# Moving the first half's large loads and one store from SyncE's DMA queue to ScalarE's

## The chip, the cores and the metric

The kernel runs on one core of one Trainium2 chip. A core has five instruction streams that run side by side and meet through semaphores: PE (TensorE, matrix products), DVE (VectorE), ACT (ScalarE), POOL (GpSimd) and SP (SyncE, which here does nothing but begin DMA transfers). Each stream executes its instructions strictly in the order in which the program has them. The metric is the device time of one execution in microseconds (us), lower is better. Three runs of the kernel before took 1967.37, 1973.29 and 1975.88 us.

## The reference

One layer, 4096 tokens of width 1024, batch 1. The token rows are normalised and modulated to `h`; one projection of `h` feeds three mixers side by side, whose outputs are gated, joined and projected back:

```
h = _rmsnorm(x, g_pre) * (1.0 + scale[:, None]) + shift[:, None]
proj = h @ w_in
...
attn = _sliding_window_attention(...)            # 8 query heads, 2 key heads, window 128, sinks
rwkv = _rwkv7_mixer(h, rr, rk, rv, ...)          # 4 heads of 64, delta rule, token by token
gla = _gla_mixer(h, gq, gkk, gv, ...)            # 4 heads, chunks
...
y = jnp.concatenate([attn, rwkv, gla], axis=-1) @ w_out
return x + gate[:, None] * _rmsnorm(y, g_post)
```

The RWKV mixer is a recurrence `S = S*w + (S @ -kk)(kk*a)^T + v k^T` over 4096 tokens. The kernel does it in chunks of 64 tokens; each chunk needs the inverse of a 64x64 triangular matrix for each head.

## The kernel before, in words

Tokens are handled in 16 tiles of 256. The program has two halves. The first half makes `h` of every tile, the RWKV and the GLA mixer, and on the side splits the weights of the second half into two 16-bit parts. The second half is attention, the gates and the output projection. `h` travels from the first half to the second through a scratch tensor in DRAM, `hscr`.

In the first half a tile passes through stages, several tiles being under way at once:

- `stage_a` loads the tile's token rows twice over: `xh`, 128 rows of 1024 at a time (512 KB, two per tile, one buffer), for the sums of squares that ACT makes, and `xt`, the same tokens with channels on the partitions (1 MB, one buffer). From `xt` ACT and DVE make `hT`, the two 16-bit halves of `h` (ACT writes the high half, DVE subtracts for the low half), and `hT` is stored to `hscr` (1 MB).
- `stage_p` projects `hT` on PE (tiles `pv`, `lp`, `zz`, `gqk`): this is most of PE's work.
- `stage_qa`, `stage_qb` and `stage_qc` build the triangular matrices `AT` and invert them. The 16x16 blocks on the diagonal go through DRAM to be laid out anew: eight transfers `adr<-AT` of 8 KB, two `AS<-adr` of 64 KB, then fifteen steps of substitution on DVE (`tsc`, `TT`), two `tdr<-TT` of 32 KB, eight `td<-tdr` of 8 KB, and then the products `Xp`, `Xq` on PE that assemble the inverse.
- `stage_q2` runs the recurrence over the tile's four chunks (`rp`, `up`, `yp`), with ACT copying `UV` between products.
- `stage_c` and `stage_g` prepare weights (`cs` loads, `wscr`, `woscr` stores, `gaw` loads).

The order of the instructions is not the order of the code. Every call goes through a recorder (`Lane`, line 352 is the line of the recorded call, so nearly all instructions bear it), and `Order.pin` then walks through the recorded steps with a table of costs, engine by engine, and fixes the order in which each engine executes them. A DMA step counts there as a step of SP with 0.47 us of SP's time and a landing time by size, all behind each other in one pipe. In the whole program all transfers but one are begun by SP, so they stand in one queue in the order of SP's stream; the one exception is a load of `gscr` at line 1598 that ACT begins at the start of the second half.

The scheduling framework gives every DMA step one of eight completion semaphores, in turn, whichever engine begins it. A step that is given a semaphore waits, before it is begun, until the step that had it last (eight DMA steps earlier) has landed. In the listings these waits read `DMAHW0_49` to `DMAHW7_49`; a wait for another engine's work bears that engine's name.

Of the kernel before, what the change touches and what calls it, by code (L numbers as in the profile page):

```python
# [21 lines left out]
P = 128  # L22
D = 1024
T = 4096
NT = 256
# [14 lines left out]
LANES = ((0.06, 1.04e-3, VL), (0.02, 1.0e-3, AL), (0.1, 2.3e-3, 0.0), (0.0, 1e-3 / 2.4, PL), (0.05, 0.0, 2.0))  # L40
# [3 lines left out]
HOP_FROM = {"PE": 0.037, "DVE": 0.034, "Activation": 0.034, "Pool": 0.06, "SP": 0.6}  # L44
HOP_INTO = {"PE": 0.02, "Pool": 0.04, "SP": 0.03}
# [20 lines left out]
class Order:  # L66
# [34 lines left out]
    def note(self, eng, name, outs, ins, func, r):  # L101

        st = Step()
# [3 lines left out]
        e, o = st.eng, outs[0]  # L107
# [3 lines left out]
        if e == "PE":  # L111
# [9 lines left out]
            cells = [4 * a + b for a in range(*rows) for b in range(*cs)]  # L121
            st.array = (mode, cells, 2 if f32 and name == "matmul" else 1, took, issue)
            st.occ = st.lat = 0.0
        elif e == "SP":
            st.bytes = math.prod(ins[0].shape) * SIZE[ins[0].dtype]
            kb = st.bytes / 1024
            st.occ = 0.47
            st.lat = next((t for k, t in ((8, 2.2), (64, 3.2), (128, 3.4), (256, 4.4), (512, 5.8)) if kb <= k), 7.5)
        elif e == "Activation":
            st.occ = (0.05 if on_psum else 0.093) + 0.093 * (len(ins) - 1) + 0.832e-3 * n  # L130
            st.lat = st.occ + 0.1
            if len(outs) > 1:
                st.occ += 0.187
                st.lat = st.occ + 0.02
            st.table = LN_TABLE if func == AF.Ln else EXP_TABLE if func in (AF.Exp, AF.Tanh) else None
        elif e == "Pool":
            if name == "memset":
                st.occ = 0.06
            elif name == "tensor_copy":
                st.occ = 0.25 if n <= 2 else 0.11 + 0.95e-3 * n  # L140
            elif n <= 8:
                st.occ = 0.33 + 0.165 * n
            else:
                st.occ = 0.42 + 1.5e-3 * n if n <= 512 else 1.85e-3 * n
            st.lat = st.occ + 0.05
        else:
            if name == "tensor_reduce":
                n = math.prod(ins[0].shape[1:])
            fast = name in ("tensor_scalar", "tensor_single_scalar") and not on_psum and o.dtype == F32
            fixed, rate = 0.065 + 0.06 * (cols > 0), 1.04e-3  # L150
            if fast:
                rate = 0.53e-3
            elif name == "transpose":
                fixed = 0.09
            elif name == "tensor_tensor_scan":
                rate = 2.08e-3
            elif name == "memset":
                fixed, rate = 0.05, 0.3e-3
            elif name == "tensor_tensor" and len(o.shape) == 3 and o.shape[2] <= 16 and n > 16:
                fixed, rate = 0.09, 1.55e-3  # L160
            st.occ = fixed + rate * n
            st.lat = st.occ + 0.085
# [7 lines left out]
            st.port = e == "Pool" and wide > 8  # L170
        k, st.needs, st.turn = len(self.steps), {}, []
        out_r, in_r = [self.region(a) for a in outs], [self.region(a) for a in ins]
        if e in ("Activation", "DVE"):

            st.half = (out_r[0][1], in_r[0][1] if e == "Activation" and in_r and out_r[0][2] - out_r[0][1] <= 64 else None)
        tiles = {a.tensor.name: a.tensor for a in [*outs, *ins]}

        if e == "SP" and self.behind is not None:
            st.turn.append(self.behind)

        def need(j, data=False):
# [51 lines left out]
    def pin(self):  # L233

        steps = self.steps
# [15 lines left out]
            if head[k] == k and not left[k]:  # L251
                ready[st.eng][k] = 0.0
        free = dict.fromkeys(ENGINES, 0.0)
        cells, mode, table, pipe, half = [0.0] * 16, None, None, 0.0, {}
        last, count, held = {}, 0, 0.0
        while count < len(steps):
            e = min((e for e in ENGINES if ready[e]), key=lambda e: max(free[e], min(ready[e].values())))
# [12 lines left out]
            for k in bursts.get(k, [k]):  # L270
# [10 lines left out]
                else:  # L281
# [9 lines left out]
                    free[e], st.end = t + st.occ, t + st.lat  # L291
                    if st.bytes:

                        pipe = max(pipe, t + 1.7) + st.bytes / 400e3
                        st.end = max(st.end, pipe)
                st.start = t
                if e in last:
                    self.tc.add_manual_dep(
                        st.ins, last[e], mybir.DependencyInfo(mybir.DependencyClass.NoSync, mybir.DependencyReason.DATA))
                last[e], count = st.ins.name, count + 1  # L300
                for q in st.then:
                    to, h = steps[q], head[q]
                    left[h] -= 1
                    at = t if k in to.turn else 0.0
                    if k in to.needs and e != to.eng:
                        at = max(at, st.end + HOP_FROM[e] + HOP_INTO.get(to.eng, 0.0))
                    elif k in to.needs and (e == "SP" or e != "PE" and to.needs[k]):
                        at = max(at, st.end + (1.2 if e == "SP" else 0.03))
                    when[h] = max(when[h], at)
                    if not left[h]:  # L310
                        ready[to.eng][h] = when[h]
# [105 lines left out]
def hybrid_kernel(ctx, tc, x, xc, rows, ada1, adaw, w1, wl, w2, wo, cst, abias, out):  # L417
# [4 lines left out]
    G = Lane(model, nc.gpsimd, *LANES[2])  # L422
    PE = Lane(model, nc.tensor, *LANES[3], serial=True)
    SP = Lane(model, nc.sync, *LANES[4])

    def pool_of(at, name, bufs=1, **kw):
        return model.order.pool(at.enter_context(tc.tile_pool(name=name, bufs=bufs, **kw)), bufs)
# [229 lines left out]
    with ExitStack() as p1:  # L657
# [60 lines left out]

        def load_tokens(i, a):
            xh = wt([P, D], "xh", 1)  # L720
            SP.dma_start(xh, x[i * NT + a * P : i * NT + (a + 1) * P, :])
            E[i]["xh"] = xh

        def load_channels(i):
            xt = E[i]["xt"] = t_x().rearrange("p a d -> p (a d)").rearrange("p (k t) -> p k t", k=KD)
            SP.dma_start(xt, xc[i])


        scolb = pp.tile([P, KD, 32], F32, name="scolb")
# [297 lines left out]
        def stage_a(i):  # L1027
# [26 lines left out]
            for kp in range(KD // 2):  # L1054
# [3 lines left out]
                S.activation(hT[:, 0, ks], xt[:, ks], AF.Identity)  # L1058
                V.tensor_sub(hT[:, 1, ks], xt[:, ks], hT[:, 0, ks])
                yield [xt]  # L1060
            SP.dma_start(hscr[i], hT.rearrange("p a k t -> p (a k t)"))

        def stage_p(i):

# [1147 lines left out]
```

## Time and profile before

| | before |
|---|---|
| three runs, us | 1967.37, 1973.29, 1975.88 |
| the profiled execution, its own time, us | 1972.81 |
| span of the profiled execution, first to last instruction, us | 1971.0 |
| PE busy in the span, us | 1875.8 (95%) |
| DVE, ACT, POOL busy, us | 1412.5, 1118.1, 375.2 |
| data moved by DMA, MB | 257.57 |

The first half occupies PE up to about 925 us of the span, the second half the rest; around the border the two overlap. In the listings of stretches, each row has a stretch of the span, its length, then for each engine its busy time and its number of instructions, then the granted clock of PE, the mean busy share of the 16 DMA engines, and the rate. In lists of waits a row says who waited, for what, and then the total, the number of waits and the longest. "SPq" and "ACTq" are the instructions by which SP and ACT begin a transfer.

### The profile page before, as it was taken

To read this page: it belongs to the slowest core of one execution; us is meant where nothing else is said; L and a number is where in the kernel's file an instruction comes from. 1 tells how busy PE (TensorE), PEld (TensorE's weight loads), DVE (VectorE), ACT (ScalarE), POOL (GpSimd) and SP (SyncE) were. 2 spreads that over 40 slices of the span, in tenths; PEclk is the share of its full clock that TensorE was granted. 3 is DMA by queue.
4 is the path that set the end of the run, shared out by engine and by line. 5 is a ranking of instruction groups with operands and counts; after the bars stand their busy time and mean duration, and the time that the engine had idled before them with its cause. 6 is when DMAs were issued, how large, how long until landed. Compare 5 with 4: busy or idle time off the path is not lost.

```text
span 1971.0 us, 59112 instructions
## 1 busy us (share of the span) xinstructions
PE 1875.8 (95%) x24651; PEld 1458.2 (74%) x24651; DVE 1412.5 (72%) x3919; ACT 1118.1 (57%) x2529; POOL 375.2 (19%) x549
## 2 busy tenths in 40 slices
PE   5799999999999999999999999999999999999997
PEld 1577788877878777877777777877778777777783
DVE  4777788888878888767638775667666676666756
ACT  4887787777777767645335443444444444344443
POOL 0533233543333344332200000000000000000001
PEclk9899999999999999999999999999999999999999
DMA  9553453443342443115244443244332444334415
GB/s 378 188 168 120 141 171 124 141 155 100 104 132 86 133 133 112 52 40 191 62 142 146 153 131 112 90 150 132 121 121 90 150 132 119 123 94 147 132 40 169
DMA packets 154264, 257.57 MB, mean 131 GB/s; under 512 B 49027, under 2 KB 100995, under 8 KB 147845
## 3 DMA queue, kind: packets, MB, share of 16 engines
q1 hardware_dynamic: 153844, 253.19, 40.2%
q8 instruction: 196, 3.21, 0.7%
q14 instruction: 80, 0.65, 0.1%
q10 hardware_dynamic: 144, 0.52, 0.1%
HBM read 192.83 MB, written 60.82 MB: 129 GB/s over the span
## 4 chain that ended last, share of the span: by engine, by line
PE 80%; DVE 6%; DMA 5%; ACT 5%; issue 3%; SPq 1%; POOL 1%; DVEq 0%; ACTq 0%; POOLq 0%
PE gp L352 17%; PE op L352 14%; PE zz L352 8%; PE qp L352 8%; PE pv L352 4%; PE lp L352 4%; PE gqk L352 3%; PE kp L352 3%; PE vp L352 2%; PE ovp L352 2%; PE sc L352 2%; PE atp L352 2%; PE yp L352 1%; PE rp L352 1%; DMA xh<-in_x 1%
## 5 line engine op out<-in xcount | busy, mean ns | idle before, releaser
L352 PEld LDWEIGHTS <-mtp 128*128 128x128 f16 x1344 | 129.2, 98 | 142.3 <-DMA ov<-woscr 3.6
L352 PE MATMUL op<-o,mtp 128*128 128x512 f16 x768 | 181.0, 380 | 0.0
L352 ACT ACTIVATE pr<-pr,nm,lsc 128x160 f32<-128x160 f32 (+2 forms) x256 | 129.1, 506 | 87.2 <-DVE nm L352 87.1
L352 PE MATMUL op<-ov,mtp 128*128 128x512 f16 x576 | 138.5, 382 | 3.8 <-DVE yv L352 2.4
L352 PEld LDWEIGHTS <-hT 128*128 128x128 f16 x1536 | 120.9, 100 | 23.8 <-ACT hT L352 4.1
L352 POOL TENSOR_TENSOR ry<-sy,expo 128x1 f32<-128x1 f32 x30 | 18.1, 619 | 537.6 <-DVE sy L352 537.6
L352 PE MATMUL pv<-gvh,hT 128*128 128x272 f16 x512 | 101.7, 290 | 5.7 <-ACT hT L352 4.0
L352 DVE TENSOR_TENSOR yv<-op,yv 128x512 f32<-128x512 f32 x105 | 70.6, 684 | 50.8 <-PE op L352 50.8
L352 DVE CUSTOM_DVE_ANT_0 pr<-sc,ab,kept 128x160 f32<-128x160 f32 (+2 forms) x256 | 85.6, 375 | 28.9 <-PE sc L352 28.8
L352 DVE SCALAR_TENSOR_TENSOR ag<-ag,gp 128x512 f32<-128x512 f32 x64 | 43.8, 684 | 80.3 <-ACT ag L352 80.1
L352 PE MATMUL gqk<-hT,gqkh 128*128 128x256 f16 x512 | 88.7, 275 | 6.6 <-DVE zb L352 6.1
L352 PE MATMUL zz<-hT,kh 128*128 128x256 f16 x512 | 94.3, 274 | 0.0
L352 PE MATMUL gp<-hT,q6h 128*128 128x256 f16 x512 | 88.7, 279 | 5.5 <-issue 5.5
L352 ACT ACTIVATE ag<-gp,gh 128x512 f32<-128x512 f32 x64 | 43.7, 683 | 88.3 <-PE gp L352 88.0
L352 PE MATMUL lp<-hT,Lh 128*128 128x256 f16 x512 | 93.4, 276 | 0.1
L352 PE MATMUL zz<-hT,rh 128*128 128x256 f16 x512 | 92.0, 275 | 0.7 <-DVE gq_s L352 0.7
L352 PE MATMUL gp<-hT,q5h 128*128 128x256 f16 x512 | 87.6, 274 | 0.0
L352 ACT ACTIVATE xt<-xt,sh,gs 128x256 f32<-128x256 f32 x128 | 70.0, 591 | 30.6 <-DVE xt L352 28.3
L352 PE MATMUL gp<-hT,q3h 128*128 128x256 f16 x512 | 87.2, 273 | 0.1
L352 PE MATMUL zz<-hT,vh 128*128 128x256 f16 x512 | 86.2, 273 | 0.0
L352 PE MATMUL qp<-hT,q0h 128*128 128x256 f16 x512 | 86.2, 273 | 0.0
L352 PE MATMUL gp<-hT,q4h 128*128 128x256 f16 x512 | 86.1, 273 | 0.0
(429 smaller groups left out, 5765.4 us busy)
## 6 DMA issues: line engine op xcount, KB each, us to landing
ov<-woscr SPq DMA_DIRECT2D x96, 512.0 KB, 5.1
xh<-in_x SPq DMA_DIRECT2D x32, 512.0 KB, 3.8
xt<-in_xc SPq DMA_DIRECT2D x16, 1024.0 KB, 8.2
hscr<-hT SPq DMA_DIRECT2D x16, 1024.0 KB, 5.6
hT<-hscr SPq DMA_DIRECT2D x16, 1024.0 KB, 4.9
x<-in_x SPq DMA_DIRECT2D x30, 512.0 KB, 4.3
out<-yv SPq DMA_DIRECT2D x30, 512.0 KB, 2.9
cs<-in_w SPq DMA_DIRECT2D x56, 256.0 KB, 4.3
```

The source lines that it names most:

```text
L352: r = f(*args, **kw)
```

## The change

The loads of `xh` and `xt` (except those of the first tile) and every store of `hscr` are begun by ACT. Nothing else of the work changes; the other transfers of the first half, those of the inverse among them, stay with SP. The planner is told of it: a DMA step begun by ACT takes its 0.47 us from ACT's time, and there are two pipes for landing times, one for SP's transfers and one for ACT's, that slow each other where they overlap. Since the planner walks through all steps with these costs, the order of every engine's instructions in the first half comes out anew. The second half's order is the same but for the steps of the first half that reach into it.

```
+    AQ = Lane(model, nc.scalar, *LANES[4])
...
         def load_tokens(i, a):
             xh = wt([P, D], "xh", 1)
-            SP.dma_start(xh, x[i * NT + a * P : i * NT + (a + 1) * P, :])
+            (AQ if i else SP).dma_start(xh, x[i * NT + a * P : i * NT + (a + 1) * P, :])
...
             xt = E[i]["xt"] = t_x().rearrange("p a d -> p (a d)").rearrange("p (k t) -> p k t", k=KD)
-            SP.dma_start(xt, xc[i])
+            (AQ if i else SP).dma_start(xt, xc[i])
...
-            SP.dma_start(hscr[i], hT.rearrange("p a k t -> p (a k t)"))
+            AQ.dma_start(hscr[i], hT.rearrange("p a k t -> p (a k t)"))
```

and in the planner:

```
-        elif e == "SP":
+        elif name == "dma_start":
             st.bytes = math.prod(ins[0].shape) * SIZE[ins[0].dtype]
             kb = st.bytes / 1024
             st.occ = 0.47
...
-                        pipe = max(pipe, t + 1.7) + st.bytes / 400e3
-                        st.end = max(st.end, pipe)
+                        begin = max(pipes[e], t + 1.7)
+                        both = max(0.0, min(max(pipes.values()) - begin, st.bytes / 400e3)) if pipes[e] < max(pipes.values()) else 0.0
+                        pipes[e] = begin + st.bytes / 400e3 + both
+                        st.end = max(st.end, pipes[e])
```

In all, 61 DMA steps move: 30 loads of `xh`, 15 of `xt`, 16 stores of `hscr`, 48 MB. What it does to the two streams is shown at three places; `L352` before and `L354` after are the same line of the recorder.

First, SP's stream around the inverse of the third tile, before:

```order
L352 DMA adr<-AT 16x8x16 x8
L352 DMA hscr<-hT 128x4096
L352 DMA cs<-in_w 128x512
L352 DMA xt<-in_xc 128x2048
L352 DMA AS<-adr 64x256 x2
```

and the same place in the change:

```order
L354 DMA adr<-AT 16x8x16 x8
L354 DMA AS<-adr 64x256 x2
L354 DMA cs<-in_w 128x512 x2
L354 DMA tdr<-TT 64x128 x2
L354 DMA td<-tdr 16x8x16 x8
```

The store of `h` and the load of `xt`, 2 MB together, no longer stand between the two steps of the inverse's layout change.

Second, ACT's stream where the load of tile 3 is begun, with what each row waits for, in the change:

```order
L354 ACTIVATE zs<-zz,mu_s 128x256 [waits PE_49,Pool_49]
L354 ACTIVATE zs<-zz,mu_s 128x256
L354 DMA xh<-in_x 128x1024 [waits DMAHW5_49]
L354 ACTIVATE ch,wss_1445<-cs 128x512 [waits DMAHW1_49]
L354 DMA xt<-in_xc 128x2048 [waits DMAHW6_49]
L354 ACTIVATE xh,ssx<-xh 128x1024 [waits DMAHW5_49]
L354 DMA xh<-in_x 128x1024 [waits DMAHW0_49,Activation_49]
L354 ACTIVATE vg<-pv,ivgv 128x256 [waits PE_49]
```

Ahead of these three in the order of DMA steps stand the eight `td` transfers of the first tile, in SP's stream of the change:

```order
L354 DMA td<-tdr 16x8x16 [waits DMAHW3_49,DMAHW2_49]
L354 DMA td<-tdr 16x8x16
L354 DMA td<-tdr 16x8x16 [waits DMAHW7_49]
L354 DMA td<-tdr 16x8x16 [waits DMAHW0_49]
L354 DMA td<-tdr 16x8x16 [waits DMAHW1_49]
L354 DMA td<-tdr 16x8x16 x2
L354 DMA td<-tdr 16x8x16 [waits DMAHW4_49]
```

They hold semaphores 5, 6, 7, 0, 1, 2, 3 and 4 in this order (each row's wait for its own semaphore is left out where it is known to have come). So ACT's rows, which wait for 5, 6 and 0, wait for the first, second and fourth of them to land. Counted over the program, 35 of the 61 moved steps are given a semaphore that a transfer of the inverse (`adr`, `AS`, `tdr`, `td`) had last.

Third, ACT's stream at the start, behind the making of the first tile's `hT`, before:

```order
L352 ACTIVATE xt<-xt,sh,gs 128x256
L352 ACTIVATE kh<-stgRA,wsc 128x1024
L352 ACTIVATE hT<-xt 128x512
L352 ACTIVATE kh<-stg,wsc 128x1024
L352 ACTIVATE rh,wss_551<-stg 128x1024
L352 ACTIVATE xh,ssx<-xh 128x1024
L352 ACTIVATE rh,wss_551<-stg 128x1024
```

and in the change:

```order
L354 ACTIVATE xt<-xt,sh,gs 128x256
L354 ACTIVATE xh,ssx<-xh 128x1024
L354 ACTIVATE hT<-xt 128x512
L354 DMA xh<-in_x 128x1024
L354 ACTIVATE kh<-stgRA,wsc 128x1024
L354 DMA hscr<-hT 128x4096
L354 DMA xt<-in_xc 128x2048
L354 ACTIVATE kh<-stg,wsc 128x1024
L354 ACTIVATE rh,wss_551<-stg 128x1024 x2
```

Three of ACT's new DMA steps stand here (a fourth, an `xh`, stands twelve rows earlier), and the first pass over the second tile's `xh` comes ahead of the last `hT` row instead of behind the first `rh` row. Further on, before the `BK<-kp` rows, ACT passed twice over the third tile's `xh`; in the change the first of these passes stands behind the first `BK` rows. The number of instructions that are not DMA steps is the same on every engine, ACT's 67 table loads among them.

More of the change, by code (lines that the diff above doesn't have):

```diff
@@ L172, in note @@
         out_r, in_r = [self.region(a) for a in outs], [self.region(a) for a in ins]
-        if e in ("Activation", "DVE"):
+        if e in ("Activation", "DVE") and not st.bytes:
             st.half = (out_r[0][1], in_r[0][1] if e == "Activation" and in_r and out_r[0][2] - out_r[0][1] <= 64 else None)
         tiles = {a.tensor.name: a.tensor for a in [*outs, *ins]}
-        if e == "SP" and self.behind is not None:
+        if st.bytes and self.behind is not None:
             st.turn.append(self.behind)
@@ L253, in pin @@
         free = dict.fromkeys(ENGINES, 0.0)
-        cells, mode, table, pipe, half = [0.0] * 16, None, None, 0.0, {}
+        cells, mode, table, pipes, half = [0.0] * 16, None, None, {"SP": 0.0, "Activation": 0.0}, {}
         last, count, held = {}, 0, 0.0
@@ L301, in pin @@
                 for q in st.then:
-                    to, h = steps[q], head[q]
+                    to, h, by = steps[q], head[q], "SP" if st.bytes else e
                     left[h] -= 1
                     at = t if k in to.turn else 0.0
[L305 to L308, printed above, removed]
+                    if k in to.needs and by != ("SP" if to.bytes else to.eng):
+                        at = max(at, st.end + HOP_FROM[by] + HOP_INTO.get(to.eng, 0.0))
+                    elif k in to.needs and (by == "SP" or e != "PE" and to.needs[k]):
+                        at = max(at, st.end + (1.2 if by == "SP" else 0.03))
                     when[h] = max(when[h], at)
```

## The prediction

> **What bounds the kernel now.** I read the page first, then the busy times by stretch, then PE's own waits in the stretches that the change can touch, and last the transfers.
>
> ```profile
> PE 1875.8 (95%) x24651; PEld 1458.2 (74%) x24651; DVE 1412.5 (72%) x3919; ACT 1118.1 (57%) x2529; POOL 375.2 (19%) x549
> ...
> 50.00:100.00 50.00, 35.67 (x273) 28.00 (x272) 36.56 (x84) 42.92 (x81) 27.78 (x35) 0.86 0.54 185
> 100.00:450.00 350.00, 342.32 (x5362) 277.70 (x5361) 281.79 (x847) 272.06 (x590) 127.26 (x187) 1.00 0.47 146
> 450.00:925.00 475.00, 462.10 (x7338) 372.25 (x7337) 383.59 (x1160) 326.39 (x696) 165.92 (x238) 0.99 0.34 103
> 925.00:1000.00 75.00, 70.13 (x1249) 54.91 (x1246) 47.01 (x188) 27.37 (x82) 14.72 (x21) 0.98 0.34 112
> ```
>
> PE bounds it. The change's edits begin near 37 us and end with the last store of `h` near 826 us. PE stands idle 50 - 35.67 = 14.3 us of the stretch 50 to 100, 350 - 342.32 = 7.7 us of 100 to 450, and 12.9 us of 450 to 925. Since PE's instructions stay the same in number and kind, these 35 us are all that a new order can win, and most of it has other causes. From 100 us on the gain is looked for in 2 to 3 percent of a stretch.
>
> PE's longest waits, from 50 to 100 us and then from 100 to 450 us:
>
> ```profile
> PE wssp L352 <- ACT gqkh L352: 4.9, 1, 4.9
> PE gqk L352 <- DVE zb L352: 4.2, 1, 4.2
> ...
> PE vp L352 <- DVE zb L352: 3.3, 1, 3.3
> PE Xp L352 <- DVE D L352: 2.6, 1, 2.6
> PE rp L352 <- DVE Ss L352: 0.7, 1, 0.7
> ```
>
> In the first stretch PE waits for weights and gates that ACT and DVE make; ACT is busy 42.92 of 50 us there. In the second only `Xp` (2.6) and `rp` (0.7) belong to the inverse and the recurrence behind it.
>
> Now the transfers: size and median time from issue to landing, from 30 to 450 us and then from 450 to 925 us.
>
> ```profile
> xh<-in_x SPq DMA_DIRECT2D x30, 512.0 KB, 3.8
> hscr<-hT SPq DMA_DIRECT2D x9, 1024.0 KB, 5.4
> xt<-in_xc SPq DMA_DIRECT2D x9, 1024.0 KB, 8.6
> AS<-adr SPq DMA_DIRECT2D x12, 64.0 KB, 4.2
> td<-tdr SPq DMA_DIRECT2D x48, 8.0 KB, 2.2
> ...
> hscr<-hT SPq DMA_DIRECT2D x7, 1024.0 KB, 5.8
> xt<-in_xc SPq DMA_DIRECT2D x6, 1024.0 KB, 7.9
> AS<-adr SPq DMA_DIRECT2D x18, 64.0 KB, 2.2
> td<-tdr SPq DMA_DIRECT2D x72, 8.0 KB, 1.8
> ```
>
> The small `AS` transfers do land later while `xh` is being loaded: 4.2 us against 2.2. That is the effect the change removes, and it exists only up to 450 us, as all `xh` loads are done by then. What does it cost? Who waited for `AS` in 100 to 430 us, and who for the `td` transfers in the whole program:
>
> ```profile
>   POOL AS L352: 27.4, 5
>   DVE tsc L352: 2.5, 2
> ...
>   DVE D L352: 0.4, 1
> ```
>
> POOL waits because its memset of `AS` stands next in its stream. DVE, which does the substitution, waited only 2.5 us for POOL's memset, and 0.4 us for all `td` transfers together: the written order already has other work where the latency falls.
>
> **The change part by part.** *The inverse, 100 to 450 us.* Six tiles have their `AS` there, 4.2 - 2.2 = 2.0 us sooner for each, 12 us of latency, of which 2.5 + 0.4 us was waited for on DVE and 2.6 + 0.7 = 3.3 us by PE behind it. SP's own waits in 30 to 450 us also leave its stream:
>
> ```profile
> SPq L352 <- ACT xh L352: 82.5, 17, 13.2
> SPq L352 <- DVE hT L352: 13.0, 3, 9.7
> ```
>
> These 95 us held up whatever stood behind in SP's stream, but by the `DVE tsc` and `DVE D` rows hardly anything of the inverse that was needed. I take 3 us, nearly all of the 3.3. Bounds: 7.7 us, all of PE's idle time in the stretch, and 0. From 450 us on `AS` lands in 2.2 us already and only `hscr` and `xt` move: 0, with a bound of a third of the 12.9 us, 4.3.
>
> *The start, 37 to 100 us.* ACT's rows there, and SP's store of the first `hT`:
>
> ```profile
> 48.45 0.61 ACT L352 ACTIVATE hT<-xt 128x512 f16<-128x512 f32 x1
> 48.97 1.13 ACT L352 ACTIVATE kh<-stg,wsc 128x1024 f16<-128x1024 f32 x1
> ...
> 58.50 1.05 ACT L352 ACTIVATE xh<-xh 128x1024 f32<-128x1024 f32 x1
> ...
> 62.40 0.63 ACT L352 ACTIVATE ch<-cs 128x512 f16<-128x512 f32 x1 [1.11 <-DMA cs<-in_w]
> ...
> 64.54 1.58 ACT L352 ACTIVATE xt<-xt,sh,gs 128x256 f32<-128x256 f32 x3 [0.68 <-DVE xt L352]
> ...
> 83.13 1.04 ACT L352 ACTIVATE xh<-xh 128x1024 f32<-128x1024 f32 x1
> 84.08 0.18 ACT L352 ACTIVATION_READ_ACCUMULATOR xh<-xh 128x1 f32 x1
> ...
> 52.64 0.39 SPq L352 DMA_DIRECT2D hscr<-hT  x1
> ```
>
> ACT is the chain here. It gains four DMA steps (two `xh`, one `hscr`, one `xt`), and at the store of `hT` it waits for DVE's half: SP could begin that store only at 52.64, ACT's half was done at 48.45 + 0.61 = 49.06, and one cast of 1.13 us lies between in the new order, so at most 2.4 us; I take half, 1.2. It loses the two idle pieces, 1.11 + 0.68 = 1.8 us, since the second tile's tokens come sooner, and two passes over `xh` with their readouts, 2 x (1.04 + 0.18) = 2.4 us, which come after 95 us.
>
> What a DMA step costs its engine is read from SP's and from the one that ACT has now:
>
> ```profile
> L352 SPq DMA_DIRECT2D xh<-in_x x32: 327/348/1407, 3.1 to 369.3; - x32
> L352 SPq DMA_DIRECT2D hscr<-hT x16: 332/356/1565, 52.6 to 826.1; - x16
> L352 SPq DMA_DIRECT2D xt<-in_xc x16: 417/444/2399, 3.5 to 775.3; - x16
> ...
> 920.34 0.84 ACT L352 ACTIVATE zs<-zz,mu_s 128x256 f32<-128x256 f32 x2
> 925.59 0.34 ACTq L1598 DMA_DIRECT2D x<-gscr  x1
> ```
>
> ACT's step took 0.34 us, like SP's medians of 0.35, 0.36 and 0.44. Four at the start are 2 x 0.35 + 0.36 + 0.44 = 1.5 us. The start comes to 1.5 + 1.2 - 1.8 - 2.4 = -1.5. Bounds: -9.1 (both long PE waits gone) and 1.5 + 2.4 = +3.9 (steps and wait, no gain).
>
> *ACT from 100 us on.* The other 57 steps cost 28 x 0.35 + 15 x 0.36 + 14 x 0.44 = 21.4 us of ACT's time. Cover: ACT is idle 78 us of 100 to 450 and 149 us of 450 to 925. Much of that is ACT waiting for PE, between 100 and 925 us:
>
> ```profile
> ACT vg L352 <- PE pv L352: 32.8, 13, 7.3
> ACT UV L352 <- PE up L352: 31.5, 26, 3.7
> ```
>
> Queued behind a waiting DMA step on ACT are the copies of `UV`, `vg` and `zs`; PE waits for those. Without cover all 21.4 us would show. I take 1 us: a step in front of a `UV` copy that is due, three times 0.35. The lower bound is 0, since no row lets ACT's extra work gain anything.
>
> *Landing times of the moved transfers.* `xt` of a tile is wanted tens of microseconds after its load, and `hscr` only in the second half; 0.
>
> Sum, against the profiled execution's own 1972.8 us (the three runs' median is 0.5 above it): 1972.8 - 3 - 1.5 + 1 = 1969.3, forecast **1969 us**, a chance of 0.33. Its own range, from spread in where the new order leaves PE waiting, is 1963 to 1976.
>
> **The rivals.** *No gain at all, 1973 us (0.21).* The queues are two, the waits stay one: 35 of the 61 moved steps take over a semaphore from a small transfer and the small ones take theirs from the large, so a `td` still waits for an `xt` eight steps earlier to land. For it: `xt` takes 8.6 us to land, longer than eight `td` steps take to begin. Against it: the 13.2 us that SP stood for one `xh` are gone whatever the semaphores do. Then the -3 falls away and the start's -1.5 is eaten by ACT's steps later on: 1972.8 - 1.5 + 1.5 = 1973.
>
> The traffic of the second queue is so far next to nothing:
>
> ```profile
> q10 hardware_dynamic: 144, 0.52, 0.1%
> ```
>
> so no row shows how two full queues share the 16 engines. [...]
>
> *Clearly faster, 1955 us (0.27).* The new order starts tile 2 sooner and closes the long waits of the start and of the first seven tiles. For it: the start is a chain through ACT and DVE, PE's idle 14.3 us there is the densest of the first half, and two waits make 9.1 us of it. Against it: the chain is work on ACT, which the change adds to. 14.3 + 7.7 = 22.0, less some 4 that pipeline fill leaves: 1972.8 - 18 = 1955.
>
> *Slower, 1987 us (0.19): ACT is held at a DMA step.* SP could afford to stand still, ACT cannot: a step whose semaphore or whose `hT` is late stops everything behind it. The place is the step that stands just after a `td` or `adr` group. For it: at its one DMA step of now ACT ended its last `zs` at 920.34 + 0.84 = 921.2 and began the step at 925.59, 4.4 us idle. Against it: mostly five or more ACT instructions stand between the last `hT` and its store. The price: half of the 21.4 us plus one wait of 4.4 us that reaches PE: 10.7 + 4.4 = 15.1, less about 1 of the start's gain: 1987. It decides from about 10 us, two or three waits of that size that reach PE.
>
> **How the numbers follow.** About 0.5%, 10 us, is what a measurement of this kernel tells from no change: below 1963 is faster, above 1983 slower. The forecast and the first rival lie between: 0.33 + 0.21 = 0.54. Faster 0.27, slower 0.19. Neither side holds enough to move the point. The range of 1953 to 1987 reaches to the faster case's 1955 with 2 us of spread and to the slower one's 1987; it leaves out the far half of either, some 0.19. All the idle time of 50 to 450 us gone would be 1951, all of ACT's steps on the path with nothing won 1972.8 + 3.9 + 21.4 = 1998.
>
> **What would show it.** In the profile after: `AS` landing near 2.2 us from 30 to 450 us (4 us speaks for the first rival); SP's wait for `ACT xh` gone, and waits of ACT for DMA or for `DVE hT` below some 10 us in total (tens would be the slower case); PE idle in 50 to 100 us down by one or two us from 14.3, and in 100 to 450 us by about 3 from 7.7; 450 to 925 us unchanged at 12.9. The forecast is wrong if PE's idle time moves by 10 us in any one of these stretches, or if the second half, whose order is the same, changes its length.

## The result, and the profile after

The changed kernel takes 1988.18 us (median of 6 runs, 1986.61 to 1998.63); the kernel before, run beside it, 1974.05 (6 runs, 1967.37 to 1980.76). The ratio is 1.0082 with a 95% interval of 1.0056 to 1.0107: slower by 0.8%, some 16 us by the ratio (the two medians lie 14 us apart). The profiled execution took 1988.72 us, its span is 1986.9. The forecast of 1969 us had the wrong sign, and 1988 lies just above the range of 1953 to 1987.

First the busy times of the page and of the same stretches, after the change; columns as in the prediction. The last row is the second half, laid 16 us later than in the row of before that it answers to (1000 to 1971 us: PE busy 938.56).

```profile
PE 1881.0 (95%) x24651; PEld 1459.5 (73%) x24651; DVE 1421.3 (72%) x3919; ACT 1119.0 (56%) x2529; POOL 373.5 (19%) x549
...
50.00:100.00 50.00, 37.19 (x261) 28.11 (x259) 37.64 (x78) 40.58 (x76) 27.69 (x39) 0.78 0.42 132
100.00:450.00 350.00, 341.02 (x5217) 276.17 (x5219) 279.84 (x839) 266.15 (x570) 121.73 (x180) 0.98 0.45 140
450.00:925.00 475.00, 457.64 (x7382) 365.42 (x7378) 381.22 (x1146) 327.15 (x707) 162.46 (x235) 0.99 0.35 108
925.00:1000.00 75.00, 68.31 (x1184) 55.04 (x1182) 53.16 (x179) 28.87 (x70) 21.40 (x27) 0.98 0.37 122
...
1016.00:1987.00 971.00, 937.38 (x10316) 715.45 (x10316) 634.90 (x1531) 424.07 (x1037) 32.18 (x49) 0.99 0.39 124
```

PE's idle time went from 1971.0 - 1875.8 = 95.2 to 1986.9 - 1881.0 = 105.9 us, and the same 24651 products kept it busy 5.2 us longer. The two add up to the 15.9 us of the span. The second has the size of the difference in the granted clock: 0.982 of full clock over 1986.9 us against 0.985 over 1971.0, so by an estimate 1986.9 x 0.018 - 1971.0 x 0.015 = 6 us of full clock more were missing. The clock differs between executions of one kernel, though (0.979 to 0.989 in those of the kernel before), so one execution of each doesn't tell how much of it is due to the change. The idle time of the stretch 50 to 100 fell by the 1.5 us of the forecast (14.3 to 12.8), that of 100 to 450 rose (7.7 to 9.0), that of 450 to 925 rose (12.9 to 17.4), and the second half has nearly the same (32.4 and 33.6).

The small transfers landed sooner in the median, from 30 to 450 us:

```profile
AS<-adr SPq DMA_DIRECT2D x12, 64.0 KB, 3.0
```

It was 4.2 us. But the median hides what counts. One pair of `AS` loads, that of the sixth tile (tile 5, counted from 0), with the transfers around it in 20 us, first before, then after (q1 is SP's queue, q10 ACT's: packets, MB, share of the 16 engines):

```profile
q1 hardware_dynamic: 3630, 3.87, 62.7%
...
hscr<-hT SPq DMA_DIRECT2D x1, 1024.0 KB
xt<-in_xc SPq DMA_DIRECT2D x1, 1024.0 KB, 7.8
...
AS<-adr SPq DMA_DIRECT2D x2, 64.0 KB, 6.4
```

```profile
q10 hardware_dynamic: 576, 3.15, 44.1%
q1 hardware_dynamic: 3177, 1.50, 29.0%
...
hscr<-hT ACTq DMA_DIRECT2D x1, 1024.0 KB
xt<-in_xc ACTq DMA_DIRECT2D x1, 1024.0 KB, 10.5
...
AS<-adr SPq DMA_DIRECT2D x2, 64.0 KB, 9.5
```

With both transfers of 1 MB gone from its queue, the pair took 9.5 us instead of 6.4, while ACT's queue moved 3.15 MB. And this pair has a wait behind it. Who waited longest between 100 and 450 us, PE first, then DVE for POOL's step on `AS` in the whole first half:

```profile
PE Xp L354 <- DVE D L354: 3.3, 1, 3.3
PE up L354 <- DVE rs L354: 3.2, 1, 3.2
```

```profile
  DVE tsc L354: 6.3, 4
```

The same row of before:

```profile
  DVE tsc L352: 3.2, 3
```

DVE's waits for `AS` have doubled, from 3.2 to 6.3 us. PE's 3.2 us for `rs` stand right behind the longest of them, at the pair of tile 5, in DVE's stream and then PE's:

```profile
406.09 0.18 DVE L354 TENSOR_TENSOR tsc<-TT,AS 128x16 f32<-128x16 f32 x1 [4.85 <-POOL AS L354]
```

```profile
406.53 0.69 PE L354 MATMUL up<-rs,tf 64*64 64x64 f32 x8 [3.24 <-DVE rs L354]
```

### The profile page after: what moved, and what is told of

It is laid out like the page before. It is cut to its first block, busy times and chain, and to the rows that moved or that the text cites. A ratio compares the mean times of both kernels' runs of the same rounds, so it can differ in the third digit from the quotient of the medians.

```text
span 1986.9 us, 59107 instructions
## 1 busy us (share of the span) xinstructions
PE 1881.0 (95%) x24651; PEld 1459.5 (73%) x24651; DVE 1421.3 (72%) x3919; ACT 1119.0 (56%) x2529; POOL 373.5 (19%) x549
## 4 chain that ended last, share of the span: by engine, by line
PE 57%; DVE 5%; DMA 4%; ACT 3%; issue 3%; POOL 1%; SPq 1%; DVEq 0%; ACTq 0%; POOLq 0%
PE gp L354 17%; PE op L354 12%; PE qp L354 8%; PE zz L354 3%; PE kp L354 2%; PE ovp L354 2%; PE vp L354 2%; DMA ov<-woscr 2%; PE sc L354 2%; PE lp L354 2%; PE pv L354 1%; PE gqk L354 1%; DVE tsc L354 1%; PE rp L354 1%; PE yp L354 1%
## 5 line engine op out<-in xcount | busy, mean ns | idle before, releaser
L354 PEld LDWEIGHTS <-mtp 128*128 128x128 f16 x1344 | 128.8, 98 | 140.9 <-DMA ov<-woscr 3.1
L354 PE MATMUL op<-o,mtp 128*128 128x512 f16 x768 | 180.6, 379 | 0.2 <-ACT q L354 0.2
L354 ACT ACTIVATE pr<-pr,nm,lsc 128x160 f32<-128x160 f32 (+2 forms) x256 | 129.1, 506 | 87.7 <-DVE nm L354 87.7
L354 PE MATMUL op<-ov,mtp 128*128 128x512 f16 x576 | 137.7, 379 | 4.2 <-DMA ov<-woscr 4.2
L354 PEld LDWEIGHTS <-hT 128*128 128x128 f16 x1536 | 121.5, 100 | 23.2 <-ACT hT L354 3.8
L354 POOL TENSOR_TENSOR ry<-sy,expo 128x1 f32<-128x1 f32 x30 | 18.1, 621 | 539.5 <-DVE sy L354 539.5
L354 DVE CUSTOM_DVE_ANT_0 pr<-sc,ab,kept 128x160 f32<-128x160 f32 (+2 forms) x256 | 85.5, 374 | 31.1 <-PE sc L354 31.1
L354 DVE TENSOR_TENSOR yv<-op,yv 128x512 f32<-128x512 f32 x105 | 70.6, 684 | 50.8 <-PE op L354 50.8
L354 PE MATMUL pv<-gvh,hT 128*128 128x272 f16 x512 | 99.8, 288 | 5.5 <-ACT hT L354 3.7
L354 DVE SCALAR_TENSOR_TENSOR ag<-ag,gp 128x512 f32<-128x512 f32 x64 | 43.8, 684 | 79.1 <-ACT ag L354 79.1
L354 PE MATMUL gqk<-hT,gqkh 128*128 128x256 f16 x512 | 90.4, 279 | 8.7 <-DVE zb L354 8.7
L354 PE MATMUL zz<-hT,rh 128*128 128x256 f16 x512 | 95.4, 281 | 2.0 <-DVE x L354 2.0
L354 ACT ACTIVATE ag<-gp,gh 128x512 f32<-128x512 f32 x64 | 43.7, 683 | 87.2 <-PE gp L354 87.0
L354 PE MATMUL lp<-hT,Lh 128*128 128x256 f16 x512 | 92.3, 278 | 0.0
L354 PE MATMUL zz<-hT,kh 128*128 128x256 f16 x512 | 91.3, 273 | 0.0
L354 PE MATMUL zz<-hT,vh 128*128 128x256 f16 x512 | 87.7, 273 | 0.0
L354 PE MATMUL gp<-hT,q6h 128*128 128x256 f16 x512 | 87.7, 278 | 0.0
L354 PE MATMUL qp<-hT,q0h 128*128 128x256 f16 x512 | 87.2, 275 | 0.0
L354 PE MATMUL gp<-hT,q3h 128*128 128x256 f16 x512 | 87.0, 273 | 0.1
L354 PE MATMUL gp<-hT,q5h 128*128 128x256 f16 x512 | 86.7, 273 | 0.0
L354 PE MATMUL gp<-hT,q4h 128*128 128x256 f16 x512 | 86.4, 273 | 0.0
```

The costliest lines, as they stand in the source:

```text
L354: r = f(*args, **kw)
```

## The experiments

Each run was compared with runs of the kernel before on the same chip (medians of 1968.9 to 1972.6 us), so the ratios are what to compare. Eighteen kernels were run.

### Apart: the written order, and who begins the steps

The change does two things: the planner writes a new order for every engine, and the steps go to another queue. The first two kernels do one each. In the first, the planner goes on taking the steps for SP's, so every other instruction keeps its place, and ACT begins them where they fall in its stream:

```
+        st.real = st.eng
+        if name == "dma_start":
+            st.eng = "SP"                    # for the plan alone
...
-            SP.dma_start(hscr[i], ...)
+            act_dma(hscr[i], ...)            # begun by nc.scalar; xh and xt likewise
```

> The planner plans exactly as before (all transfers counted on SP, one pipe), so PE, DVE, ACT and POOL have their instructions in the order of before; only the 61 steps are begun by ACT, set into its stream where the old plan had them on SP. If ACT's new steps or the second queue cost the time (theory A, my slower rival), this is as slow as the change: about 1988 us, ratio 1.005 to 1.010. If the new written order costs it (theory B), about 1974 us or some 1 to 4 us less, ratio 0.998 to 1.001.

Measured 1990.46 us, ratio 1.0098 (1.0072 to 1.0124). The second keeps the changed kernel's plan, and SP begins all steps:

```
+    AQ.issue = nc.sync
```

> The planner plans exactly as in the change, so the four computing engines have their instructions in the change's order; but all 61 steps are begun by SP, in its one queue, at the places in time that the plan gives them. Theory A: the loss goes with ACT's steps, so about 1974 us, ratio 0.998 to 1.002. Theory B: the loss goes with the order, about 1985 to 1995 us, ratio 1.005 to 1.011.

Measured 1981.24 us, ratio 1.0046 (1.0027 to 1.0066). So both parts cost, some 19 and 9 us by the ratios. They don't add: the change with both costs 16, so in its own order ACT's beginning the steps adds only some 7 us, give or take 6 by the two intervals.

Two readings of the section above change with these kernels. The wait at tile 5 belongs to the new plan and not to the second queue: the plan puts the store of `h` and the load of `xt` ahead of this pair whoever begins them. With SP beginning all steps the pair took up to 9.2 us as well, and DVE's waits for `AS` in the first half came to 4.9 us, 4.6 of them at tile 5:

```profile
  DVE tsc L355: 4.9, 2
...
DMA to landing us min/median/max: 2.0/2.9/9.2
```

And the median of 3.0 us from 30 to 450 us is the new plan's: it is 3.1 with SP beginning all steps, while in the order of before, with all 61 steps on ACT, it is not below the 4.2 of before:

```profile
AS<-adr SPq DMA_DIRECT2D x12, 64.0 KB, 4.9
```

Whether a redrawn order costs by itself was tried on the kernel before, by one constant of its planner:

```
-            st.occ = 0.47
+            st.occ = 0.43                    # second run: 0.50
```

> The kernel before, with one cost of the planner changed that nothing on the chip follows: a DMA step takes 0.43 us of SP in the plan and not 0.47. It draws a new written order. Theory C, that any redrawn order moves the time by several us either way and the change drew a bad one: 1963 to 1985 us, likely more than 5 us from before. Theory B in its narrow form, that this change's order alone is bad because it counts on a second pipe: within 3 us of before.

> As the kernel before it, with 0.50 us in the plan and not 0.47: a second draw of the order. Theory C: again 1963 to 1985 us, and not the same as the other draw. Theory B, narrow: within 3 us of before.

Measured 1982.77 us, 1.0052 (1.0032 to 1.0071), and 1995.08 us, 1.0120 (1.0088 to 1.0152). A redrawn order costs 10 or 24 us with nothing else changed: the order of before is better than both redraws, and the change gave it up.

### What of ACT's beginning them costs: ACT's time or the queue

Four kernels with the written order of before on all engines. In the first SP begins all steps, and ACT has a copy of 128x240 numbers in the place of each of the 61:

```
+        r = nc.scalar.activation(pads[k], first[:, 0:240], AF.Identity)
         SP.dma_start(dst, src)
+        model.order.steps[-1].pair = r.ins   # stands in ACT's stream where the step would
```

> Written order of before on every engine and every transfer begun by SP; in ACT's stream, at each of the 61 places where the old order with ACT's steps had a step, a copy of 128x240 numbers stands instead, whose result nobody reads (by the rows of 128x8, 0.21 us, and 128x512, 0.62 us, about 0.40 us each, 24 us in all, against 26.4 us of the steps). Theory D, ACT's time: the steps cost because what stands behind them on ACT is late and PE waits for it; then the copies cost nearly what the steps cost, 1985 to 1992 us, and PE's added waits stand at copies of UV. Theory E, the second queue: the cost is made by the transfers and their semaphores; then the copies cost 0 to 4 us, 1972 to 1977 us.

The next two let ACT begin one group only (`act_dma` for `xh`, or for `xt` and `hscr`; the other as before), the last gives the 61 steps to POOL:

```
-        SP.eng = nc.scalar
+        SP.eng = nc.gpsimd
```

> Written order of before, ACT begins the 30 loads of xh (all before 370 us), SP the rest. Theory D: a share of the 18 us by ACT's time before 370 us, where ACT is idle 22 percent of the time: 7 to 10 us, 1980 to 1983 us. Theory E: the loads of xh are what the inverse's small transfers met, so this half gains, if any does: 1968 to 1973 us.

> Written order of before, ACT begins the 15 loads of xt and the 16 stores of h, SP the rest. Theory D: the other share of the 18 us, 8 to 11 us, 1980 to 1984 us. Theory E: nearly all of the 18 us, as these are the transfers of 1 MB: 1986 to 1992 us.

> Written order of before, the 61 steps begun by POOL, which is busy 375 of 1971 us: a queue of their own without ACT's time. Theory D: little, as POOL has the time and PE hardly waits for it: 1970 to 1977 us, less if the AS transfers landing sooner are worth something. Theory E: the cost of a second queue shows here as well: 1985 to 1992 us. If a step of POOL takes a microsecond or more, up to 61 us of POOL, both are weakened, and the rows of POOL tell.

Measured: the copies 1974.60 us, 1.0010 (0.9995 to 1.0025); `xh` alone 1976.42, 1.0020 (1.0001 to 1.0040); `xt` and `h` 1986.31, 1.0078 (1.0053 to 1.0103); POOL 1980.71, 1.0057 (1.0033 to 1.0082). Theory D falls: 24 us more of ACT's time cost between -1 and 5 us, and a queue begun by POOL, which takes nothing from ACT, costs 6 to 16. (What POOL's own time has in that is not separated: worked out from its trace, its 61 steps took 0.59 us each in the median, 36 us in all, and it stood 22.5 us waiting for DVE's half of `hT` ahead of the stores.) The transfers of 1 MB carry it.

Where `xt` and `h` are ACT's, the pair of `AS` loads of tile 5 shows what is different. ACT's stream:

```profile
390.51 0.26 ACT L355 COPY UV<-up 64x128 f32<-64x128 f32 x1 [0.23 <-PE up L355]
390.77 0.34 ACTq L355 DMA_DIRECT2D hscr<-hT  x1
390.80 0.26 ACT L355 COPY UV<-up 64x128 f32<-64x128 f32 x1
...
391.42 0.38 ACTq L355 DMA_DIRECT2D xt<-in_xc  x1
```

SP's stream at the same place before:

```profile
390.62 0.46 SPq L352 DMA_DIRECT2D hscr<-hT  x1
391.25 2.20 SPq L352 DMA_DIRECT2D AS<-adr  x2
393.49 1.20 SPq L352 DMA_DIRECT2D cs<-in_w  x1
394.73 0.46 SPq L352 DMA_DIRECT2D xt<-in_xc  x1
```

Before, the load of `xt` stood behind the pair, which SP took 2.20 us to begin, and behind a load of `cs`: it began at 394.73. ACT begins it at 391.42, 3.3 us sooner, while the pair is under way. ACT itself loses next to nothing here: a copy of `UV` begins at 390.80, while the step is still shown as running, and behind both steps, at its next `gw`, ACT is 0.29 us later than in the kernel before (391.59 against 391.30), as it already was ahead of them by 0.28 (390.51 against 390.23).

The reading is theory F, overtaking: SP's one stream had kept 1 MB back behind 128 KB that are waited for, and a second queue no longer does. Theory G, its rival, has the cost in the step itself (ACT held at it, some steps of 1 to 2 us).

### Overtaking or the step

Four kernels, again with the order of before. In the first, ACT begins 61 transfers of 4 KB that nobody reads, in the places of the steps, and SP the 61 real ones:

```
+        r = nc.scalar.dma_start(pads[k], cst[:, 0:8])
         SP.dma_start(dst, src)
```

> As the run with copies in the place of ACT's steps (1974.6 us), but each copy is now a transfer of 4 KB begun by ACT, whose data nobody reads; the 61 real transfers are begun by SP as before. So ACT has the 61 steps of a second queue, without their traffic. Theory F, overtaking: what costs is the traffic, since the 1 MB that stood behind the AS loads in SP's stream (8 places) now runs beside them; then these steps cost as little as the copies, 1973 to 1978 us. Theory G, the step itself: ACT stands at a step and takes some steps 1 to 2 us, which a copy does not; then most of the 18 us comes back, 1985 to 1992 us.

In the second ACT begins `xt` and `h`, but those near a pair of `AS` loads later:

```
+        for st in [st for st in row if st.tag in ("hscr<-hT", "xt<-in")]:
+            near = [t for t in pairs if -6.0 <= t - st.start <= 12.0]
+            if near:   # behind the first step of ACT that the plan has 6 us behind the pair
+                at = row.index(st)
+                to = next(q for q in range(len(row)) if row[q].start > near[-1] + 6.0 and q > at)
+                row.insert(to - 1, row.pop(at))
```

> As the run in which ACT begins xt and h (1986.3 us), but each of the 17 steps that the plan has from 12 us ahead of a pair of AS loads to 6 us behind it (9 stores of h, 8 loads of xt) stands in ACT's stream 6 us behind that pair. Every other order is that of before. Theory F: AS lands in 3 us or so at these tiles, and the cost of 14 us falls to 0 to 5 us: 1972 to 1978 us. Theory G: the 31 steps on ACT cost the same wherever they stand: 1983 to 1990 us.

The third does the like in SP's own stream, with nothing on ACT (tile 2 of its eight tiles is shown), and the fourth gives ACT the stores of `h` alone:

```
-hscr<-hT
 cs<-in_w
-xt<-in_xc
 AS<-adr x2
+hscr<-hT
+xt<-in_xc
```

```
-            SP.dma_start(hscr[i], ...)
+            act_dma(hscr[i], ...)
```

> The kernel before with one edit in SP's own stream, no second queue: the 13 steps for h and xt that stand up to 12 us ahead of a pair of AS loads (8 stores of h, 5 loads of xt) are put right behind that pair. Theory F: AS lands about 2 to 4 us sooner at eight tiles; PE waits for the inverse only in part of them, so the time is that of before or a little lower, 1966 to 1973 us, and DVE's wait for AS falls from 3.2 us to about 0. Theory G says nothing of it: 1972 us. If the stores that come later hold up the buffers of hT or the next tile's xt, it is slower, above 1977 us.

> Written order of before, ACT begins the 16 stores of h only; the loads of xt stay in SP's stream, so where they stood behind the AS loads they still do. Theory F: the stores stood ahead of AS on SP too, at all places but one, so little changes: 1972 to 1977 us. Theory G: 16 of the 31 steps of xt and h, about half of their 14 us: 1978 to 1981 us.

Measured: the small transfers 1974.66 us, 1.0000 (0.9980 to 1.0020); behind `AS` 1974.07, 1.0004 (0.9988 to 1.0019); SP alone, behind `AS` 1971.36, 0.9992 (0.9976 to 1.0008); `h` alone 1970.78, 1.0001 (0.9980 to 1.0021). All four as theory F has it, and theory G falls twice: the steps cost nothing without their traffic, and 31 real steps cost nothing once 17 of them stand 6 us behind a pair. ACT's own time at them had not shrunk: worked out from the traces, its 32 steps there took 18.5 us with 0.2 us of idle time ahead of the 31, against 14.8 and 3.2 us where they cost 15 us. The pair of tile 5 in that kernel:

```profile
hscr<-hT ACTq DMA_DIRECT2D x1, 1024.0 KB, 4.9
...
AS<-adr SPq DMA_DIRECT2D x2, 64.0 KB, 2.7
```

2.7 us against 9.5 in the changed kernel and 6.4 before. That the pair can be so much faster, and the kernel no faster than before, also sizes the gain that the change was able to bring: in SP's own reordering DVE waited 0.4 us for `AS` in the whole first half instead of 3.2, and the time changed by -0.08%, which is no difference.

### The counter-proof: the same harm without a second queue

Two more kernels with the order of before. In one ACT begins the loads of `xt` alone (`act_dma(xt, xc[i])`). In the other nobody but SP begins anything; three loads of `xt` and one store of `h` that stand up to 6 us behind a pair of `AS` loads in SP's stream are put right ahead of it. Tile 5:

```
 hscr<-hT
+xt<-in_xc
 AS<-adr x2
 cs<-in_w
-xt<-in_xc
```

> Written order of before, ACT begins the 15 loads of xt only; the stores of h stay with SP. Theory F: the loads of xt that stood behind AS in SP's stream now run beside the store of h and AS, so this half carries the 14 us of xt and h together: 1981 to 1987 us. If it takes both on the second queue to hurt, 1972 to 1977 us.

> The kernel before with one edit in SP's stream alone, no second queue: at the three places where a load of xt stands up to 6 us behind a pair of AS loads (tiles 3, 5 and 10) it is put right ahead of that pair, with the one store of h that stands there too. Theory F: what costs is 1 MB moving ahead of or beside the AS loads, not the queue it comes from; the AS loads of these three tiles land 2 to 5 us later, and 5 to 12 us of time follow, 1976 to 1984 us, with PE's longest new waits in these tiles. If the second queue itself is needed for the harm: 1969 to 1974 us.

Measured 1987.51 us, 1.0087 (1.0065 to 1.0108), and 1982.66 us, 1.0063 (1.0041 to 1.0086). Four steps moved in one stream, and 12 us are gone. So the harm needs no second queue: it is enough that 1 MB stands ahead of the pair. PE's idle time agrees. From 100 to 450 us it was 7.7 us before; it is 13.9 with `xt` put ahead in SP's stream, 14.2 with `xt` on ACT, and 7.3 where ACT's steps stand behind the pairs. The rows in this order (length, PE's busy time, clock, DMA share, rate):

```profile
100.00:450.00 350.00, 336.14 (x5225) 0.99 0.46 141
...
100.00:450.00 350.00, 335.85 (x5144) 0.98 0.45 138
...
100.00:450.00 350.00, 342.67 (x5379) 1.00 0.47 146
```

The chain can be read at tile 3. Before, in POOL's stream, then in DVE's:

```profile
291.67 0.13 POOL L352 MEMSET AS<- 128x16 f32 x1 [1.35 <-DMA AS<-adr]
```

```profile
292.21 0.15 DVE L352 TENSOR_REDUCE wss<-wss 128x1 f32<-128x4 f32 x1
292.27 0.17 DVE L352 TENSOR_TENSOR tsc<-TT,AS 128x16 f32<-128x16 f32 x1
292.36 0.28 DVE L352 SCALAR_TENSOR_TENSOR Gpk<-kvp,egp,Gpk 128x64 f32<-128x64 f32 x1
```

With `xt` ahead of the pair, POOL, DVE, PE and PE's clock:

```profile
296.77 0.12 POOL L367 MEMSET AS<- 128x16 f32 x1 [6.44 <-DMA AS<-adr]
```

```profile
292.23 0.15 DVE L367 TENSOR_REDUCE wss<-wss 128x1 f32<-128x4 f32 x1
296.93 0.18 DVE L367 TENSOR_TENSOR tsc<-TT,AS 128x16 f32<-128x16 f32 x1 [4.55 <-POOL AS L367]
297.02 0.28 DVE L367 SCALAR_TENSOR_TENSOR Gpk<-kvp,egp,Gpk 128x64 f32<-128x64 f32 x1
```

```profile
297.35 0.32 PE L367 MATMUL kvp<-vg,kt 128*32 128x64 f32 x8 [3.68 <-DVE Gpk L367]
```

```profile
298.70:302.10 3.40, 3.40 (x39) 2.40 (x39) 3.30 (x20) 2.87 (x7) 0.10 (x1) 0.52 0.00 0
302.10:305.50 3.40, 3.40 (x55) 2.94 (x48) 2.88 (x20) 2.54 (x6) 0.00 (x0) 0.98 0.47 124
```

Before, `AS` was ready at 291.67 + 0.13 = 291.80, and DVE came for it at 292.27: 0.5 us to spare. 5.1 us later is 4.55 us of waiting. What PE needs is not `tsc` but `Gpk`, of another mixer, which stands behind it in DVE's stream, so PE waits 3.68 us, and then runs at half its clock for 3.4 us (granted 0.52). The first `pv` product of tile 5, worked out from the traces of the two kernels, comes 5.4 us later than before; the tiles 7 and 8 add 6.4, two and three tiles behind the pair of tile 5, and tile 12 adds 2.4, two behind that of tile 10. At the last tile it is 14.9 us, of which 5 are made up later: the profiled span is 9.7 us longer.

Which queue the 1 MB came from made little difference to the pair of tile 5: it took 8.7 us with `xt` ahead of it in its own queue and 9.7 with `xt` beside it in ACT's, in the rows below of the kernels that put `xt` ahead and that give `xt` alone to ACT.

```profile
AS<-adr SPq DMA_DIRECT2D x2, 64.0 KB, 8.7
```

```profile
q10 hardware_dynamic: 144, 1.05, 18.5%
...
xt<-in_xc ACTq DMA_DIRECT2D x1, 1024.0 KB, 9.9
...
AS<-adr SPq DMA_DIRECT2D x2, 64.0 KB, 9.7
```

The pair of `AS` isn't the only transfer that it hits, and DVE's waits for `AS` don't rank the kernels: they came to 8.8 us where `xh` alone is ACT's, which cost 4 us, and to 5.0 where `xt` and `h` are, which cost 15. In the kernel with `xt` on ACT, between 700 and 765 us, ACT, then DVE behind it, then PE:

```profile
ACT ch L355 <- DMA woscr<-ch: 4.4, 1, 4.4
```

```profile
DVE ch L355 <- ACT ch L355: 4.2, 1, 4.2
```

```profile
PE rp L355 <- DVE Ss L355: 3.3, 1, 3.3
```

A store that must land before ACT may write the buffer again is late, and the lateness goes through two streams to PE.

### How far this explains the changed kernel

One kernel applies the cure to the changed kernel itself (its own plan, ACT's steps near a pair 6 us behind it), two draw its plan anew with other constants, and one gives the kernel before the second of these constants:

```
-            st.occ = 0.47
+            st.occ = 0.43
...
-  ... st.bytes / 400e3
+  ... st.bytes / 390e3
```

> The changed kernel (1988 us) with its own plan on every engine; only those of ACT's steps for h and xt that the plan has from 12 us ahead of a pair of AS loads to 6 us behind it (6 stores, 8 loads) stand 6 us behind that pair in ACT's stream. Theory F, overtaking: what ACT's beginning adds to the new order falls away, so the time is that of the new order begun by SP, 1981 us, or a little less: 1976 to 1983 us. If the order is what costs in the changed kernel and overtaking has no part in it, 1986 to 1991 us.

> The changed kernel with the planner's cost of a step at 0.43 instead of 0.47 us: another draw of its order, to be held against the kernel before with the same constant (1982.8 us). Theory H: any redrawn order lies 5 to 20 us above before's, whatever begins the steps, and overtaking adds 3 to 15 us on top in most orders: 1984 to 1998 us. If the changed kernel's order is what is bad and not the redrawing: within 3 us of 1983.

> The changed kernel with the planner's rate of transfers at 390 instead of 400 KB/us: a third draw of its order. Theory H as above: 1980 to 1998 us, on no side of 1988 for certain. A time below 1972 would show that a redrawn order can gain as well.

> The kernel before with the planner's rate of transfers at 390 instead of 400 KB/us, all steps begun by SP: the partner of the changed kernel with that constant (1994.0 us, 1.25 percent over before). Theory H: a redrawn order, 5 to 20 us above before, and below its partner by what ACT's beginning costs, 3 to 15 us: 1976 to 1990 us. If the change does harm only by the order that it drew, the two are within 3 us: 1991 to 1997 us.

| planner's constants | before, ratio | changed, ratio |
|---|---|---|
| as given (0.47 us, 400 KB/us) | 1 | 1.0082 (1.0056 to 1.0107) |
| step 0.43 us | 1.0052 (1.0032 to 1.0071) | 1.0147 (1.0120 to 1.0174) |
| rate 390 KB/us | 1.0037 (1.0020 to 1.0055) | 1.0125 (1.0098 to 1.0151) |

In all three draws the changed kernel is 0.8 to 0.95% above its partner (1.0147 / 1.0052 = 1.0095, 1.0125 / 1.0037 = 1.0088). So the loss belongs to the change, its new planning and its queue together, and not to one unlucky plan, while the 7 to 24 us by which redrawn orders of the old kernel lie above it show how much an order alone is worth. None of the redrawn orders came out below the order as given.

The cure brought the changed kernel to 1980.35 us, 1.0063 (1.0039 to 1.0087). The time lies in the range expected of overtaking, but by the ratio it is halfway between the 1.0046 of the same order begun by SP and the 1.0082 of the changed kernel, and its interval holds both, so the time doesn't settle it. In the profile of the cured kernel DVE waits for `AS` in one place instead of four:

```profile
  DVE tsc L369: 0.2, 1
```

With hardly a wait for `AS` left, this kernel is still 0.63% slower than before, clear of no change. PE's idle time, in one execution of each, points the same way: between 100 and 450 us the cure takes it from 9.0 to 7.4 us, back to the 7.7 of before, but between 450 and 925 us, where it had risen from 12.9 to 17.4, it stays at 18.4. So overtaking is shown in the order of before; that it makes the larger part of the changed kernel's loss is not shown, and the runs speak rather for the new order. How the 16 us divide stays open, and so does what in the new orders costs: the waits of the kernels that were only redrawn stand at many places, and in one of them (step 0.50 us, 24 us slower) DVE hardly waits for `AS` at all (0.5 us).

## Why the prediction was wrong

**The bound and the 35 us.** Right: PE bounds the kernel before and after, busy 95% of either span.

**The start, -1.5.** Not confirmed. PE's idle time from 50 to 100 us fell by 14.3 - 12.8 = 1.5 us, as summed, but no time came of it: the granted clock of that stretch fell from 0.86 to 0.78, and the first `pv` product of the second tile came at 105.9 us, not sooner than the 104.0 of before. Nor can one execution tell a term of this size: the kernels with `xt` put ahead of the pairs and with `h` and `xt` put behind them, whose steps there are those of before, had this product at 105.7 and 103.1.

**ACT from 100 us on, +1.** Right, in the order of before. The 61 steps in their places cost 0.00% with an interval of 4 us to either side (small transfers), 24 us of copies cost 0.10%. ACT's idle time covers them, as the rows on `UV` and `vg` had it.

**Rival 1, no gain at all.** The rival fails on the time, but the mark named for it, `AS` still landing near 4 us, is what the order of before shows beside a second queue (4.2 with `xt` on ACT, 4.9 with all 61 steps); in the changed kernel it was 3.0. What moved the landing was where the large transfers stand: at tile 5 it took 9.2 to 9.7 us with `xt` beside the pair, and 2.7 with `xt` behind it. The shared semaphores that it named do not carry the loss in the order of before: SP's waits for landings between 100 and 925 us came to 35.7 us before and to 37.7 with `xt` and `h` on ACT. In the changed kernel they came to 53.9, and what those cost was not tested.

**The slower rival, 1987 us.** Right in the number, wrong in the mechanism. ACT is not held: worked out from the trace after, it stood 9.4 us in all ahead of its 62 steps, 2.9 of them ahead of the one that it had before, under the 10 us named as the point from which this case would decide. In the order of before 31 real steps cost nothing once they stand behind the pairs, and the small transfers cost nothing. Reaching 1988 us was luck for this rival.

**The faster rival, 1955 us.** No run shows the 4 us that it takes off for pipeline fill. Of the 22.0 us of idle time that it counts, 21.8 were still there after (12.8 and 9.0).

**The failed step: the inverse, 100 to 450 us, -3, and with it "Landing times of the moved transfers: 0".** The text took each `AS` pair to land 2.0 us sooner because the large loads leave SP's queue, and took 0 as the worse bound. Leaving the queue did not bring that: with the order kept, the median was 4.9 us with all 61 steps on ACT and 4.2 with `xt` alone. The text looked at the large transfers that stand *ahead* of small ones and not at those that stand *behind* them. At tiles 3, 5 and 10 SP's order held `xt` back behind the pair; where one stream put it ahead, the pair was ready 5, 2.4 and 7 us later by the traces. The diff's first place showed a tile where the planner drew the good case; tile 5, where the new plan itself puts `xt` ahead of the pair, wasn't looked up. Measured, in the order of before: +15 to +17 us for `xt` on ACT, with `h` or alone, in place of -3; in the changed kernel's own order some +7, give or take 6, for ACT's beginning the steps.

**The cover, read wrongly.** From `DVE tsc 2.5` and `DVE D 0.4` the text concluded that "the written order already has other work where the latency falls". The cover was there but 0.5 us thick at tile 3. A wait of nearly 0 says that a transfer is in time; it doesn't say by how much. Sooner gained nothing (-0.08%), later cost at once, and more than the lateness of the work itself, since what waited in the end was `Gpk` behind it in DVE's stream.

**The spread of a redrawn order.** Priced at 1963 to 1976. Redrawing the old kernel alone gave 1977.7, 1982.8 and 1995.1 us, and the changed plan begun by SP 1981.2. This is the second step that failed: a new written order stood at 0 in the sum and measured +9, no less than the other part of the loss. Why a redrawn order costs so much stays open.

**What would show it.** SP's wait for `xh` is gone, as said. The second half kept its length within 3 us (959.0 and 961.6 us from ACT's first `mxa` to the end), as said. `AS` landed in 3.0 us in the median, not near 2.2; PE's idle time was to fall by 3 us from 100 to 450 us and rose by 1.3, and was to stay from 450 to 925 us and rose by 4.5. It moved by 1.5, 1.3 and 4.5 us in the three stretches and in none by 10, so the test set for a wrong forecast didn't strike although the forecast was wrong: the loss was spread, and a third of it is PE's longer busy time and not idle time.

## What to carry to other kernels

In these runs a transfer's place in one issuing stream was a priority: the pair of tile 5 took 6.4 us with `xt` behind it in SP's stream and 8.7 with `xt` ahead of it. Before moving large transfers to another queue, list for each the small ones that stand right behind it *and* those right ahead of it, and ask for each of these how long before its first use it lands. Read the margin from the two time stamps, of the landing and of the first user, since a list of waits shows 0 for a margin of 0.5 us and of 50. Where the instruction order comes from a planner, redraw the old kernel once or twice with a constant shifted by a few per cent before believing a difference of 1%: here that alone moved it by 0.4 to 1.2%.

## What the runs showed of the hardware that was not expected

Two waits of PE cost more than their length. At tile 3 of the kernel with `xt` put ahead, PE waited 3.68 us and then ran 3.40 us at a granted 0.52. In the changed kernel a wait of 3.24 us, at tile 5, had more behind it:

```profile
400.00:412.00 12.00, 8.76 (x101) 6.51 (x100) 6.45 (x23) 5.47 (x13) 5.43 (x11) 0.72 0.56 195
```

Here 12.00 x (1 - 0.72) = 3.4 us of full clock are missing. In finer stretches the granted clock is 1.00 from 400 to 405 us, 0.50 from 405.2 to 412.0 and 0.94 in the 0.2 us behind that: it fell while PE still waited, and for the 5.5 us from the end of the wait at 406.53 to 412.0 PE ran at half its clock. What made it fall, and what raised it again, is not shown.

In the kernel with `xt` and `h` on ACT, ACT is shown computing while it begins a transfer: the step at 390.77 lasts 0.34 us, and a copy begins at 390.80. Which of the two stands first in ACT's stream the trace doesn't tell. It isn't so at every step: in the changed kernel the next instruction comes 0.04 us behind the end of the step at 101.60, and 0.10 us behind that of the step at 134.59.
